# Gates and branch outputs of a hybrid mixer by rows, 512 weight columns at a time, and a transposed merge

## The chip, the cores and the metric

The kernel runs on one core of one Trainium2 chip. The metric is the device time of one execution in microseconds, median of three runs. Five engines work side by side: TensorE (PE in the rows; its weight loads are PEld), VectorE (DVE), ScalarE (ACT), GpSimd (POOL), and SyncE (SP), which issues the DMA transfers here.

## The reference, cut to what matters

Two layers work on 256 tokens of 1024 channels in fp32. In each, the mixer combines an attention branch and a Hyena branch (long convolutions) by sigmoid gates:

```python
y_att = o_att.astype(u.dtype) @ w_o_attn            # (256, 512) @ (512, 1024)
...
y_hy = z @ w_o_hyena                                # (256, 1024) @ (1024, 1024)
gates = jax.nn.sigmoid((u @ w_gate + b_gate).astype(jnp.float32)).reshape(B, S, N_BRANCH, D_MODEL)
merged = gates[:, :, 0] * y_att.astype(jnp.float32) + gates[:, :, 1] * y_hy.astype(jnp.float32)
return merged.astype(u.dtype) @ w_out               # (256, 1024) @ (1024, 1024)
```

`w_gate` has 2048 columns. A normalisation, a residual, and a SwiGLU block follow.

## The kernel before

**Products.** Every fp32 operand `x` of a large product is split into a rounded part `hi` and a remainder `lo`, and a product is three matmuls that add up in one PSUM bank, hi·hi, hi·lo and lo·hi (`mm3`, L80). The activations are kept transposed, channels on partitions, as pairs such as `UH`, `UL` (normalised input), `ZH`, `ZL` (Hyena), `OTH`, `OTL` (attention) and `MH`, `ML` (merged).

**Weights.** They come in pieces of 128 x 1024 (`raw`, 512 KB, four buffers, `RAW`), issued by SP in the order of use. ScalarE rounds a piece (`whi`, L86), VectorE forms the remainder (`wlo`, L89), and every fifth remainder goes to GpSimd (`POOL_LO`). `piece()` keeps three split pieces ahead of TensorE (`AHEAD`).

**Order.** TensorE's order is the program's. On the other engines a scheduler sets it. The mixer runs, in this order: q, k and v of two head slots; 24 pieces of Hyena projections; 16 pieces of gates; two more head slots; 8 pieces of the Hyena output; 4 pieces of the attention output; 8 pieces of the output projection. After almost every piece `tick()` advances up to two background generators by a step: the attention of a slot (`attend`, L609), the convolutions of a channel block (`conv`, L538), or the filters.

**Gates and outputs by columns.** For each block of 128 output columns (`c`), the weight piece is the stationary operand or the moving one in 128 x 128 blocks, and the result is a bank of 128 channels x 256 tokens. Gates: `UH`/`UL` and `whi`/`wlo` give 24 matmuls of 256 columns, and ScalarE applies the sigmoid with the bias of the channel (`bgt`) from the bank into `GT` (L725). The Hyena output multiplies its half of the gates (L750). The attention output, half a piece for a block, multiplies the other half (L766), GpSimd adds both (L767), ScalarE and VectorE split the sum into `MH` and `ML`, and `row_proj` (L429) uses these as stationary operand, with 512 columns of weights moving. There the first two pieces serve both halves of the tokens, the last six the first half first and the second half later.

Of the kernel before, what the change touches and what calls it, by code (L numbers as in the profile page):

```python
# [20 lines left out]
F32 = mybir.dt.float32  # L21
# [6 lines left out]
P = 128  # L28
D = 1024
L = 256  # L30
# [14 lines left out]
def trunk(tc, nc, a, out):  # L45
# [4 lines left out]
    with es:  # L50
# [11 lines left out]
        def bigt(dt=F32, name="big"):  # L62
            return big.tile([P, 1024], dt, tag="big", bufs=22, name=name)
# [16 lines left out]
        def mm3(o, lh, ll, rh, rl, start, stop):  # L80
            mm(o, lh, rh, start, False)
            mm(o, lh, rl, False, False)
            mm(o, ll, rh, False, stop)
# [111 lines left out]
        rope = cst.tile([P, 2, 2, 48], F32, name="rope")  # L195
        mask = cst.tile([P, 2, 512], BF16, name="mask")
        cw = cst.tile([P, DEPTH, 24, 4], F32, name="cw")
        bgt = cst.tile([P, DEPTH, 16], F32, name="bgt")
        fpar = cst.tile([P, DEPTH, 4], F32, name="fpar")
        fc = bigt(name="fc")  # L200
        zT = fc[0:33, 0:256]
# [7 lines left out]
        def load_filter_consts():  # L209
            nc.sync.dma_start(zT, a["zT"])  # L210
            nc.sync.dma_start(fw1, a["fw1"])
            nc.sync.dma_start(fw2, a["fw2"])
            nc.sync.dma_start(fpar, a["fpar"])
            nc.sync.dma_start(bgt, a["bg"])

        def load_consts():
            nc.sync.dma_start(cw, a["cw"])
# [203 lines left out]

        def rows_of(U, o, i, pc, kk, n):

            for k in range(2):
                kt = 2 * kk + k
                w = slice(k * n, (k + 1) * n)
                mm3(o[:, :n], *u_cols(U, kt, i), pc[0][:, w], pc[1][:, w], kt == 0, kt == KT - 1)

        def row_proj(l, n, left, gn, nxt):  # L429


            banks = [[acc() for h in range(2)] for i in range(2)]
            g = g2 = None

            def part(k, i, pc, lr, hs=(0, 1)):
                for h in hs:
                    mm3(banks[i][h], lr[0][:, i * P:(i + 1) * P], lr[1][:, i * P:(i + 1) * P],
                        pc[0][:, HALF[h]], pc[1][:, HALF[h]], k == 0, k == n - 1)

            held = []  # L440
            tail = TAIL if nxt else LAST
            for k in range(n):
                shared[0] = k < n - tail - 2
                pc, lr = piece(), left(k)
                part(k, 0, pc, lr)
                if k < n - tail:
                    part(k, 1, pc, lr)
                    done(pc)
                    tick()
                else:  # L450
                    held.append((k, pc, lr))
                if k == max(0, n - tail - 3):
                    g, g2 = gain(l, gn), gain(*nxt) if nxt else None
            with ordered():
                ss = new_sums()
                for h in range(2):
                    square_sum(ss, h, banks[0][h])
                r = rstd_of(ss)
                if nxt:
                    split_hi()  # L460
                    for q in range(RAW + 1):
                        load(q >= RAW)
                    split_hi()
                add_to_x(0, [times_gain(banks[0][h], g, h) for h in range(2)], r)
                if nxt:
                    split_lo()
                    r = x_rstd(0)
                    split_lo()
                    u0 = pre_b(0, r, g2)
                else:  # L470
                    nc.sync.dma_start(out[0:P, :], X[0])
                ss, t, U = new_sums(), [], None
                for h in range(2):
                    for k, pc, lr in held:
                        if nxt and h and k == n - 2:
                            U = new_U()
                            to_cols(0, u0, U)
                        part(k, 1, pc, lr, (h,))
                    square_sum(ss, h, banks[1][h])
                    t.append(times_gain(banks[1][h], g, h))  # L480
                for _, pc, _ in held:
                    done(pc)
                r = rstd_of(ss)
                if not nxt:
                    add_to_x(1, t, r)
                    for s in HALF:
                        nc.sync.dma_start(out[P:2 * P, s], X[1][:, s])
                    return None, None

                def second():  # L490
                    split_hi()
                    add_to_x(1, t, r)
                    split_lo()
                    ss2 = new_sums()
                    for h in range(2):
                        square_sum(ss2, h, X[1][:, HALF[h]])
                    split_hi()
                    r2 = rstd_of(ss2)
                    split_lo()
                    return pre_b(1, r2, g2)  # L500

                S = start(U, second)
                shared[0] = True
                return U, S
# [168 lines left out]
        def mixer(l, U, o, K):  # L673
# [46 lines left out]

                queue.append(both())

            GT = [bigt(name="GT") for h in range(4)]
            for c in range(16):
                nc.scalar.activation(ct(GT, c), col_proj(U), AF.Sigmoid, bias=bgt[:, l, c:c + 1])  # L725
                tick()
            ZH, ZL = [], []

            def z_split():
# [9 lines left out]
                att = slot(s, [bigt(name="qk") for i in range(2)], z_split if s == 3 else None)  # L739
                queue.append(att)  # L740

            for c in range(8):
                pc = piece()
                wh, wl = pc[:2]
                o = acc()
                for k in range(KT):
                    s = slice(k * P, (k + 1) * P)
                    mm3(o[:, :L], wh[:, s], wl[:, s], ct(ZH, k), ct(ZL, k), k == 0, k == KT - 1)
                done(pc)
                vtt(ct(GT, 8 + c), ct(GT, 8 + c), o[:, :L], op=OP.mult)  # L750
                tick()
            drain()
            MH = [bigt(F32R, name="MH") for h in range(2)]
            ML = [bigt(F32R, name="ML") for h in range(2)]
            for c in range(8):
                if c % 2 == 0:
                    pc = piece()
                    wh, wl = pc[:2]
                o = acc()
                for k in range(4):  # L760
                    s = slice((c % 2) * 512 + k * P, (c % 2) * 512 + (k + 1) * P)
                    mm3(o[:, :L], wh[:, s], wl[:, s], ct([OT[0]], k), ct([OT[1]], k), k == 0, k == 3)
                if c % 2:
                    done(pc)
                g0 = ct(GT, c)
                vtt(g0, g0, o[:, :L], op=OP.mult)  # L766
                ptt(g0, g0, ct(GT, 8 + c), op=OP.add)  # L767
                hi_of(ct(MH, c), g0)
                lo_of(ct(ML, c), g0, ct(MH, c))
            return row_proj(l, KT, lambda k: (ct(MH, k), ct(ML, k)), 1, (l, 2))  # L770


        def ffn(l, U, o):
# [28 lines left out]
            def left(f):  # L802
                hs = r512("hs") if f % 2 else sm.tile([P, 512], F32R, tag="hs", bufs=5, name="hs")
                hi_of(hs[:, :L], ct(HF, f))
                lo_of(hs[:, L:], ct(HF, f), hs[:, :L])
                return hs[:, :L], hs[:, L:]

            return row_proj(l, NF, left, 3, (l + 1, 0) if l + 1 < DEPTH else None)

# [84 lines left out]
    return w.reshape(k // P, P, n // P, P).transpose(2, 1, 0, 3).reshape(n // P, P, k)  # L894


def _pack(i):
    d = _tables()
    d["x"] = np.ascontiguousarray(i["x"][0][PERM])
# [4 lines left out]
    for l in range(DEPTH):  # L904
        win = i["w_in"][l]
        hv, x1, x2 = (_col_pieces(win[:, 4608 + q * D:4608 + (q + 1) * D]) for q in range(3))
        for cc in range(4):
            c = slice(2 * cc, 2 * cc + 2)
            wa[l, PC_H + 6 * cc:PC_H + 6 * cc + 6] = np.concatenate([hv[c], x1[c], x2[c]])
        wa[l, PC_G:PC_G + 16] = _col_pieces(i["w_gate"][l])  # L910
        wa[l, PC_OH:PC_OH + 8] = _col_pieces(i["w_o_hyena"][l])
        wa[l, PC_OA:PC_OA + 4] = _col_pieces(i["w_o_attn"][l]).reshape(4, 2, P, 512).transpose(0, 2, 1, 3).reshape(
            4, P, 1024)
        wa[l, PC_OUT:PC_OUT + 8] = i["w_out"][l].reshape(8, P, D)
        gu = i["w_gate_up"][l].reshape(D, 2, D_FF)
        wg[l] = gu[:, :, :384].reshape(4, 2, P, 2, 384).transpose(3, 0, 2, 1, 4).reshape(8, P, 768)
        for q in range(2):
            wa[l, PC_GU + q:PC_DN:2] = _col_pieces(gu[:, q, 384:])
        wa[l, PC_DN:PC_DN + NF] = i["w_down"][l].reshape(NF, P, D)
        q = win[:, :4608].reshape(4, 2, P, 3, 3, 4, P)  # L920
        wq[l] = q.transpose(5, 3, 0, 2, 1, 4, 6).reshape(48, P, 768)
    d["wa"], d["wq"], d["wg"] = wa, wq, wg
    cwb = np.concatenate([i["conv_w"], i["conv_b"][:, None, :]], 1)
    d["cw"] = np.ascontiguousarray(cwb.reshape(DEPTH, 4, 24, P).transpose(3, 0, 2, 1))
    d["bg"] = np.ascontiguousarray(i["b_gate"].reshape(DEPTH, 16, P).transpose(2, 0, 1))
    fp = np.stack([i["filt_b1"], i["filt_freq1"], i["filt_b2"], i["filt_freq2"]], -1)
    d["fpar"] = np.ascontiguousarray(np.concatenate([fp, fp], 1).transpose(1, 0, 2))
    d["fw1"] = np.ascontiguousarray(i["filt_w1"].transpose(1, 0, 2))
# [31 lines left out]
```

## Time and profile before

| | us |
|---|---|
| median of three runs | 1107.41 (1107.06 to 1108.79) |
| the profiled execution | 1109.53 |
| its span, first to last instruction | 1107.6 |
| TensorE matmul busy in it | 1083.8 |
| VectorE, ScalarE, GpSimd busy | 709.9, 557.1, 396.9 |

Busy time of matmuls is modelled and overlaps, so what one costs is read from the distance between the starts of neighbours. Of layer 0, the gates (with the convolutions' steps among them) lie at 176 to 240 us, the Hyena output at 308 to 337, the attention output at 337 to 349, the output projection from 349 on.

### The profile page before, as it was taken

What the parts mean: (1) busy time and instruction counts of PE and PEld (TensorE: products, weight loads), DVE (VectorE), ACT (ScalarE), POOL (GpSimd) and SP (SyncE); (2) the same over time, 40 slices, a digit from 0 to 9 for tenths busy, and PEclk for the clock granted to TensorE, in tenths of its full rate; (3) what the DMA queues carried; (4) which work ended last, traced back from release to release, by engine and by line L of the source; (5) the groups of instructions that cost most, each with busy time, mean ns of one, the idle gap of its engine ahead of it and who ended that gap; (6) DMA issues with size and microseconds to landing.
All of it is one profiled execution on the core that took longest, in us unless ns stands there. A gap on an engine that the chain in (4) does not pass through costs nothing.

```text
span 1107.6 us, 19530 instructions
## 1 busy us (share of the span) xinstructions
PE 1083.8 (98%) x7624; PEld 1039.0 (94%) x7624; DVE 709.9 (64%) x1139; ACT 557.1 (50%) x852; POOL 396.9 (36%) x488
## 2 busy tenths in 40 slices
PE   8989999999999999999999999999999999999997
PEld 6989999999899899998879899999999989999986
DVE  5799985556647756665474877865545586554554
ACT  6555564443545645454464564454356455544442
POOL 2643133468614134211115714455645230111110
PEclk9999999999999999999999999999999999999999
DMA  8565544434446555656655454444355475465662
GB/s 295 174 211 193 159 138 134 133 117 128 148 143 201 186 188 185 192 182 223 193 169 165 144 166 134 136 151 131 122 162 196 149 232 190 151 183 182 197 199 79
DMA packets 59878, 187.21 MB, mean 169 GB/s; under 512 B 6919, under 2 KB 9353, under 8 KB 59786
## 3 DMA queue, kind: packets, MB, share of 16 engines
q1 hardware_dynamic: 59786, 185.96, 52.6%
q8 instruction: 60, 0.98, 0.4%
q14 instruction: 32, 0.26, 0.1%
HBM read 184.89 MB, written 1.05 MB: 168 GB/s over the span
## 4 chain that ended last, share of the span: by engine, by line
PE 87%; DVE 6%; DMA 3%; ACT 2%; issue 1%; POOL 1%; SPq 0%; DVEq 0%; POOLq 0%; ACTq 0%
PE acc L78 84%; DVE wlo L89 2%; PE acc L617 1%; DVE dl L89 1%; ACT whi L86 1%; DVE dd L315 1%; DMA mask<-in_mask_dram 1%; DMA raw<-in_wq_dram 1%; ACT jk L352 1%; DMA raw<-in_wa_dram 1%; PE acc L647 1%; PE acc L548 1%; PE acc L397 1%; DVE arg L241 0%; DMA w<-in_w_dram 0%
## 5 line engine op out<-in xcount | busy, mean ns | idle before, releaser
L86 ACT ACTIVATE whi<-raw 128x1024 fp32r<-128x1024 f32 (+1 forms) x352 | 345.4, 989 | 384.5 <-PE acc L78 292.6
L89 DVE TENSOR_TENSOR wlo<-raw,whi 128x1024 fp32r<-128x1024 f32 (+1 forms) x294 | 346.4, 1186 | 231.7 <-ACT whi L86 229.2
L78 PE MATMUL acc<-UH,whi 128*128 128x256 f32 x1248 | 356.0, 285 | 0.0
L78 PE MATMUL acc<-UH,wlo 128*128 128x256 f32 x1248 | 353.1, 283 | 0.0
L78 PE MATMUL acc<-UL,whi 128*128 128x256 f32 x1248 | 353.0, 283 | 0.0
L89 POOL TENSOR_TENSOR wlo<-raw,whi 128x1024 fp32r<-128x1024 f32 (+1 forms) x58 | 133.3, 2298 | 412.1 <-ACT whi L86 412.0
L78 PEld LDWEIGHTS acc<-UL,whi 128*128 128x128 f32 x1248 | 239.3, 192 | 0.4
L78 PEld LDWEIGHTS acc<-UH,whi 128*128 128x128 f32 x1248 | 239.2, 192 | 0.4
L78 PEld LDWEIGHTS acc<-UH,wlo 128*128 128x128 f32 x1248 | 239.2, 192 | 0.0
L78 PE MATMUL acc<-wlo,UH 128*128 128x384 f32 x448 | 152.4, 340 | 2.4 <-DVE wlo L89 1.3
L78 PE MATMUL acc<-whi,UH 128*128 128x384 f32 x448 | 153.8, 343 | 0.0
L78 PE MATMUL acc<-whi,UL 128*128 128x384 f32 x448 | 151.1, 337 | 0.0
L78 PE MATMUL acc<-whi,hs 128*128 128x512 f32 x352 | 108.9, 389 | 0.0
L78 PEld LDWEIGHTS acc<-wlo,UH 128*128 128x128 f32 x448 | 85.3, 190 | 5.7 <-DVE wlo L89 4.1
L78 PEld LDWEIGHTS acc<-whi,UH 128*128 128x128 f32 x448 | 85.5, 191 | 1.3 <-ACT whi L86 0.4
L78 PEld LDWEIGHTS acc<-whi,UL 128*128 128x128 f32 x448 | 85.1, 190 | 0.2 <-DVE UL L89 0.2
L78 PEld LDWEIGHTS acc<-whi,hs 128*128 128x128 f32 x352 | 66.1, 188 | 13.6
L78 PE MATMUL acc<-wlo,hs 128*128 128x512 f32 x176 | 68.6, 390 | 0.5 <-DVE wlo L89 0.5
L799 DVE TENSOR_TENSOR HF<-acc,silu 128x256 f32<-128x256 f32 x38 | 16.1, 424 | 49.1 <-PE acc L78 49.1
L359 POOL TENSOR_SCALAR nv<-ss 128x1 f32<-128x1 f32 x16 | 7.0, 440 | 103.7 <-ACT jk L352 103.7
L78 PEld LDWEIGHTS acc<-wlo,hs 128*128 128x128 f32 x176 | 33.0, 188 | 7.7 <-DVE wlo L89 0.9
L89 DVE TENSOR_TENSOR hs<-HF,hs 128x256 fp32r<-128x256 f32 x44 | 31.1, 724 | 10.3 <-ACT hs L86 10.3
(165 smaller groups left out, 1678.9 us busy)
## 6 DMA issues: line engine op xcount, KB each, us to landing
raw<-in_wa_dram SPq DMA_DIRECT2D x240, 512.0 KB, 3.6
raw<-in_wq_dram SPq DMA_DIRECT2D x96, 384.0 KB, 3.2
raw<-in_wg_dram SPq DMA_DIRECT2D x16, 384.0 KB, 3.8
w<-in_w_dram SPq DMA_DIRECT2D x16, 256.0 KB, 4.3
gain<-in_gains_dram SPq DMA_DIRECT2D x7, 512.0 KB, 6.2
dec<-in_dec_dram SPq DMA_DIRECT2D x8, 256.0 KB, 3.8
bb<-in_hyb_dram SPq DMA_DIRECT2D x16, 128.0 KB, 4.0
dftraw<-in_dft_dram SPq DMA_DIRECT2D x3, 256.0 KB, 4.4
```

What stands on the lines that cost most here:

```text
L78: nc.tensor.matmul(o, lT, r, start=start, stop=stop)
L86: return nc.scalar.activation(o, i, AF.Copy)
L89: (eng or nc.vector).tensor_tensor(o, i, h, op=OP.subtract)
L315: vtt(d[:, q * 256:(q + 1) * 256], h[:, q * 256:(q + 1) * 256], dec[:, e, :], op=OP.mult)
L352: nc.scalar.activation(jk, half, AF.Square, scale=D ** -0.5, accum_out=ss[:, h:h + 1])
L359: nc.gpsimd.tensor_scalar(v, ss[:, 0:1], ss[:, 1:2], EPS, op0=OP.add, op1=OP.add)
L397: nc.tensor.transpose(t[:, q * P:(q + 1) * P], u[:, h * 512 + q * P: h * 512 + (q + 1) * P], ident)
L548: nc.tensor.transpose(t[:, q * P:(q + 1) * P], eo[:, q // 2, q % 2, :], ident)
L617: nc.tensor.transpose(t[:, q * P:(q + 1) * P], qk[i][:, j * 384 + g * P: j * 384 + (g + 1) * P], ident)
L647: nc.tensor.transpose(t[:, q * P:(q + 1) * P], S[:, i * 512 + q * P:i * 512 + (q + 1) * P], ident)
L799: vtt(ct(HF, f), ob, sl, op=OP.mult)
```

## The change

The gates, the Hyena output and the attention output are computed by rows. Two banks hold 128 tokens x 512 columns each, one for each half `i` of the tokens; 128 x 128 blocks of the activations are the stationary operand and 512 columns of weights move. A piece of weights covers 256 input channels x 512 columns, so four pieces make a chunk of gates or of the Hyena output and two a chunk of the attention output. The bias is now a row, loaded with the same value for all partitions (`gb`, 256 KB, two buffers shared with the filters' decay windows `dec`), which VectorE adds from the bank into `GT`; ScalarE applies the sigmoid there. The merged sum lies with tokens on partitions and is turned by TensorE (`turn`), 8 transposes for each half of the columns; ScalarE and VectorE split the transposed bank into `MH` and `ML`. The first half is turned inside the last attention piece, the second before the third piece of the output projection. The bytes of weights and the number of ticks stay.

```diff
-            GT = [bigt(name="GT") for h in range(4)]
-            for c in range(16):
-                nc.scalar.activation(ct(GT, c), col_proj(U), AF.Sigmoid, bias=bgt[:, l, c:c + 1])
-                tick()
+            GT = [[bigt(name="GT") for i in range(2)] for b in range(2)]
+            for c in range(4):
+                gb = sm.tile([P, 512], F32, tag="dec", bufs=2, name="gb")
+                nc.sync.dma_start(gb, a["bg"][l, c * 512:(c + 1) * 512].partition_broadcast(P))
+                o = [acc() for i in range(2)]
+                for kk in range(4):
+                    pc = piece()
+                    for i in range(2):
+                        rows_of(U, o[i], i, pc, kk, 512)
+                    done(pc)
+                    tick()
+                for i in range(2):
+                    gt = GT[c // 2][i][:, HALF[c % 2]]
+                    vtt(gt, o[i], gb, op=OP.add)
+                    nc.scalar.activation(gt, gt, AF.Sigmoid)
...
-            for c in range(8):
-                pc = piece()
-                wh, wl = pc[:2]
-                o = acc()
-                for k in range(KT):
-                    s = slice(k * P, (k + 1) * P)
-                    mm3(o[:, :L], wh[:, s], wl[:, s], ct(ZH, k), ct(ZL, k), k == 0, k == KT - 1)
-                done(pc)
-                vtt(ct(GT, 8 + c), ct(GT, 8 + c), o[:, :L], op=OP.mult)
-                tick()
+            for c in range(2):
+                o = [acc() for i in range(2)]
+                for kk in range(4):
+                    pc = piece()
+                    for i in range(2):
+                        rows(lambda k: [ct(T, k)[:, i * P:(i + 1) * P] for T in (ZH, ZL)], o[i], pc, kk, 512, KT)
+                    done(pc)
+                    tick()
+                for i in range(2):
+                    g1 = GT[1][i][:, HALF[c]]
+                    vtt(g1, g1, o[i], op=OP.mult)
             drain()
...
+            def turn(c):
+
+                M[c] = bigt(F32R, name="MH"), bigt(F32R, name="ML")
+                for i in range(2):
+                    t = acc()
+                    for q in range(4):
+                        nc.tensor.transpose(t[:, q * P:(q + 1) * P],
+                                            GT[0][i][:, c * 512 + q * P:c * 512 + (q + 1) * P], ident)
+                    h, lo = (x[:, HALF[i]] for x in M[c])
+                    hi_of(h, t)
+                    lo_of(lo, t, h)
+
+            for c in range(2):
+                o = [acc() for i in range(2)]
+                for kk in range(2):
                     pc = piece()
...
+                    for i in range(2):
+                        if c and kk and i:
+                            turn(0)
+                        rows(lambda k: [T[:, k * L + i * P:k * L + (i + 1) * P] for T in OT], o[i], pc, kk, 512, 4)
                     done(pc)
...
+                for i in range(2):
+                    g0 = GT[0][i][:, HALF[c]]
+                    vtt(g0, g0, o[i], op=OP.mult)
+                    ptt(g0, g0, GT[1][i][:, HALF[c]], op=OP.add)
+
+            def merged(k):
+                if k == 2:
+                    turn(1)
+                return [x[:, :].rearrange("p (i q n) -> p i q n", i=2, q=4)[:, :, k % 4, :] for x in M[k // 4]]
+
+            return row_proj(l, KT, merged, 1, (l, 2))
```

What this does to the order of the instructions is seen at three places of layer 0. TensorE before, at the end of the attention output and the start of the output projection:

```order
L78 MATMUL acc<-OTH,whi 128x256
L78 MATMUL acc<-OTL,whi 128x256
L78 MATMUL acc<-OTH,wlo 128x256
L78 MATMUL acc<-whi,MH 128x512
L78 MATMUL acc<-wlo,MH 128x512
```

And in the changed kernel, where `ident` is the identity matrix of a transpose:

```order
L78 MATMUL acc<-whi,OTL 128x512
L774 MATMUL acc<-ident,GT 128x128 x8
L78 MATMUL acc<-whi,OTH 128x512
L78 MATMUL acc<-wlo,OTH 128x512
L78 MATMUL acc<-whi,OTL 128x512
L78 MATMUL acc<-whi,OTH 128x512
L78 MATMUL acc<-wlo,OTH 128x512
L78 MATMUL acc<-whi,OTL 128x512
L78 MATMUL acc<-whi,MH 128x512
L78 MATMUL acc<-wlo,MH 128x512
```

Six matmuls of the attention output stand between the first eight transposes and the output projection that needs their result. VectorE before, from the last Hyena product (L750) through the attention output:

```order
L750 TENSOR_TENSOR GT<-GT,acc 128x256
L766 TENSOR_TENSOR GT<-GT,acc 128x256 x2
L89 TENSOR_TENSOR wlo<-raw,whi 128x1024
L766 TENSOR_TENSOR GT<-GT,acc 128x256
L89 TENSOR_TENSOR ML<-GT,MH 128x256
L766 TENSOR_TENSOR GT<-GT,acc 128x256
```

The same place in the changed kernel, from the last Hyena products (L764) to the second half of the merge:

```order
L764 TENSOR_TENSOR GT<-GT,acc 128x512 x2
L89 TENSOR_TENSOR wlo<-raw,whi 128x1024
L791 TENSOR_TENSOR GT<-GT,acc 128x512 x2
L89 TENSOR_TENSOR wlo<-raw,whi 128x1024 x2
L791 TENSOR_TENSOR GT<-GT,acc 128x512
L89 TENSOR_TENSOR ML<-acc,MH 128x512 x2
L791 TENSOR_TENSOR GT<-GT,acc 128x512
L89 TENSOR_TENSOR wlo<-raw,whi 128x1024 x3
L89 TENSOR_TENSOR ML<-acc,MH 128x512 x2
```

The remainder of the first half (`ML`) stands behind two weight splits and behind the multiply (L791) of the second chunk's first half of tokens. On SP's queue the bias rows stand among the weights (`raw`), the filters' windows (`dec`) and biases (`bb`); before:

```order
L284 DMA w_1521<-in_w_dram 128x512
L287 DMA dec<-in_dec_dram 128x512
L291 DMA bb<-in_hyb_dram 128x256
L140 DMA raw<-in_wa_dram 128x1024
L291 DMA bb<-in_hyb_dram 128x256
L140 DMA raw<-in_wa_dram 128x1024 x4
L287 DMA dec<-in_dec_dram 128x512
```

And in the changed kernel:

```order
L282 DMA w_1519<-in_w_dram 128x512
L727 DMA gb<-in_bg_dram 128x512
L289 DMA bb<-in_hyb_dram 128x256
L140 DMA raw<-in_wa_dram 128x1024
L289 DMA bb<-in_hyb_dram 128x256
L140 DMA raw<-in_wa_dram 128x1024 x4
L727 DMA gb<-in_bg_dram 128x512
```

The two loads of layer 1's windows moved behind the gates' weights, and two bias rows stand in their place.

## Rows read from the trace of the kernel before

**Rows 1.** The page: busy us (share of the span) x instructions.

```profile
PE 1083.8 (98%) x7624; PEld 1039.0 (94%) x7624; DVE 709.9 (64%) x1139; ACT 557.1 (50%) x852; POOL 396.9 (36%) x488
```

**Rows 2.** Windows of layer 0: busy us by engine, granted clock, DMA share, GB/s.

```profile
176.00:240.00 64.00, 64.00 (x526) 63.97 (x525) 33.04 (x52) 28.27 (x44) 34.03 (x36) 1.00 0.42 130
...
300.00:320.00 20.00, 17.62 (x131) 17.31 (x130) 10.38 (x14) 8.49 (x13) 2.69 (x2) 0.91 0.45 147
320.00:338.00 18.00, 18.00 (x154) 18.00 (x154) 9.68 (x19) 7.35 (x11) 2.54 (x3) 1.00 0.49 157
338.00:349.00 11.00, 11.00 (x93) 11.00 (x92) 8.21 (x13) 5.50 (x9) 8.28 (x7) 1.00 0.43 144
349.00:369.00 20.00, 20.00 (x89) 16.54 (x89) 16.25 (x21) 12.61 (x22) 5.83 (x7) 1.00 0.80 259
```

**Rows 3.** The chain that ended last, layer 1: start us, us, what.

```profile
852.46 0.87 PE acc L617 x8
853.33 2.87 PE acc L78 x24
```

**Rows 4.** Timeline of TensorE, layer 0: start us, us, instruction.

```profile
337.31 0.28 PE L78 MATMUL acc<-OTH,whi 128*128 128x256 f32 x1
...
348.71 0.28 PE L78 MATMUL acc<-OTH,wlo 128*128 128x256 f32 x1
348.83 0.40 PE L78 MATMUL acc<-whi,MH 128*128 128x512 f32 x1
...
369.26 1.31 PE L397 MATMUL acc<-ident,u 128*128 128x128 f32 x8
```

**Rows 5.** Groups by shape: xcount | busy us, mean ns | idle before, releasers.

```profile
L86 ACT ACTIVATE whi<-raw 128x1024 fp32r<-128x1024 f32 x240 | 252.7, 1059 | 301.9 <-PE acc L78 226.9 <-issue 63.0 <-DMA raw<-in_wa_dram 4.2
L89 DVE TENSOR_TENSOR wlo<-raw,whi 128x1024 fp32r<-128x1024 f32 x197 | 247.9, 1264 | 154.5 <-ACT whi L86 152.1 <-issue 2.0
...
L367 DVE TENSOR_TENSOR pn<-acc,gain 128x512 f32<-128x512 f32 x16 | 11.0, 691 | 9.0 <-ACT jk L352 9.0
...
L89 DVE TENSOR_TENSOR UL<-acc,UH 128x512 fp32r<-128x512 f32 x16 | 10.6, 688 | 1.2 <-ACT UH L86 0.7 <-PE acc L397 0.2
...
L86 ACT ACTIVATE UH<-acc 128x512 fp32r<-128x512 f32 x16 | 9.1, 596 | 10.0 <-PE acc L397 9.4 <-PE acc L78 0.5
```

**Rows 6.** Instructions on GT: xcount, ns min/median/max, first and last start.

```profile
L725 ACT ACTIVATE GT<-acc,bgt x32: 453/457/475, 178.1 to 790.9; 128x256 f32<-128x256 f32 x32
...
L767 POOL TENSOR_TENSOR GT<-GT x16: 737/924/1732, 340.9 to 892.0; 128x256 f32<-128x256 f32 x16
L86 ACT ACTIVATE MH<-GT x16: 400/417/419, 341.7 to 893.7; 128x256 fp32r<-128x256 f32 x16
L89 DVE TENSOR_TENSOR ML<-GT,MH x16: 411/633/960, 343.0 to 894.2; 128x256 fp32r<-128x256 f32 x16
```

**Rows 7.** Timelines of VectorE, GpSimd and TensorE around 300 us.

```profile
298.59 0.48 DVE L639 TENSOR_SCALAR S<-S,rd 128x512 f32<-128x512 f32 x1
...
300.72 1.99 DVE L639 TENSOR_SCALAR S<-S,rd 128x512 f32<-128x512 f32 x1
...
299.87 2.55 POOL L89 TENSOR_TENSOR wlo<-raw,whi 128x1024 fp32r<-128x1024 f32 x1 [0.73 <-ACT whi L86]
...
299.52 0.33 PE L78 MATMUL acc<-wlo,UH 128*128 128x384 f32 x1
299.70 0.34 PE L78 MATMUL acc<-whi,UL 128*128 128x384 f32 x1
...
302.85 1.09 PE L647 MATMUL acc<-ident,S 128*128 128x128 f32 x4 [2.38 <-DVE S L639]
303.59 0.67 PE L78 MATMUL acc<-whi,UH 128*128 128x384 f32 x1
304.06 0.52 PE L78 MATMUL acc<-wlo,UH 128*128 128x384 f32 x1
...
305.66 0.43 PE L78 MATMUL acc<-whi,UH 128*128 128x384 f32 x1
```

More of the change, by code (lines that the diff above doesn't have):

```diff
@@ L197, in trunk @@
         cw = cst.tile([P, DEPTH, 24, 4], F32, name="cw")
-        bgt = cst.tile([P, DEPTH, 16], F32, name="bgt")
         fpar = cst.tile([P, DEPTH, 4], F32, name="fpar")
@@ L213, in load_filter_consts @@
             nc.sync.dma_start(fpar, a["fpar"])
-            nc.sync.dma_start(bgt, a["bg"])
         def load_consts():
@@ L422, in rows_of, with rows @@
         def rows_of(U, o, i, pc, kk, n):
+            rows(lambda k: u_cols(U, k, i), o, pc, kk, n, KT)
+        def rows(left, o, pc, kk, n, kts):
             for k in range(2):
@@ L426, in rows_of @@
                 w = slice(k * n, (k + 1) * n)
-                mm3(o[:, :n], *u_cols(U, kt, i), pc[0][:, w], pc[1][:, w], kt == 0, kt == KT - 1)
+                mm3(o[:, :n], *left(kt), pc[0][:, w], pc[1][:, w], kt == 0, kt == kts - 1)
         def row_proj(l, n, left, gn, nxt):
@@ L436, in part @@
                 for h in hs:
-                    mm3(banks[i][h], lr[0][:, i * P:(i + 1) * P], lr[1][:, i * P:(i + 1) * P],
+                    mm3(banks[i][h], lr[0][:, i, :], lr[1][:, i, :],
                         pc[0][:, HALF[h]], pc[1][:, HALF[h]], k == 0, k == n - 1)
@@ L740, in mixer @@
                 queue.append(att)
-            for c in range(8):
-                pc = piece()
-                wh, wl = pc[:2]
-                o = acc()
-                for k in range(KT):
-                    s = slice(k * P, (k + 1) * P)
-                    mm3(o[:, :L], wh[:, s], wl[:, s], ct(ZH, k), ct(ZL, k), k == 0, k == KT - 1)
-                done(pc)
-                vtt(ct(GT, 8 + c), ct(GT, 8 + c), o[:, :L], op=OP.mult)
-                tick()
-            drain()
-            MH = [bigt(F32R, name="MH") for h in range(2)]
@@ L754, in mixer @@
-            ML = [bigt(F32R, name="ML") for h in range(2)]
-            for c in range(8):
-                if c % 2 == 0:
-                    pc = piece()
[L758 to L763, printed above, removed]
-                    done(pc)
[L765 to L769, printed above, removed]
@@ L770, in mixer @@
-            return row_proj(l, KT, lambda k: (ct(MH, k), ct(ML, k)), 1, (l, 2))
+            for c in range(2):
[9 more added lines that the diff above has]
+                    vtt(g1, g1, o[i], op=OP.mult)
@@ new lines, in mixer @@
+            drain()
+            M = [None, None]
+            def turn(c):
[8 more added lines that the diff above has]
+                    lo_of(lo, t, h)
@@ L805, in left @@
                 lo_of(hs[:, L:], ct(HF, f), hs[:, :L])
-                return hs[:, :L], hs[:, L:]
+                return [x.rearrange("p (i n) -> p i n", i=2) for x in (hs[:, :L], hs[:, L:])]
             return row_proj(l, NF, left, 3, (l + 1, 0) if l + 1 < DEPTH else None)
@@ L894, in _col_pieces, with _row_pieces @@
     return w.reshape(k // P, P, n // P, P).transpose(2, 1, 0, 3).reshape(n // P, P, k)
+def _row_pieces(w):
+    k, n = w.shape
+    return w.reshape(k // 256, 2, P, n // 512, 512).transpose(3, 0, 2, 1, 4).reshape(k * n // (P * 1024), P, 1024)
 def _pack(i):
@@ L909, in _pack @@
             wa[l, PC_H + 6 * cc:PC_H + 6 * cc + 6] = np.concatenate([hv[c], x1[c], x2[c]])
[L910 to L913, printed above, removed]
+        wa[l, PC_G:PC_G + 16] = _row_pieces(i["w_gate"][l])
+        wa[l, PC_OH:PC_OH + 8] = _row_pieces(i["w_o_hyena"][l])
+        wa[l, PC_OA:PC_OA + 4] = _row_pieces(i["w_o_attn"][l])
         wa[l, PC_OUT:PC_OUT + 8] = i["w_out"][l].reshape(8, P, D)
@@ L924, in _pack @@
     d["cw"] = np.ascontiguousarray(cwb.reshape(DEPTH, 4, 24, P).transpose(3, 0, 2, 1))
-    d["bg"] = np.ascontiguousarray(i["b_gate"].reshape(DEPTH, 16, P).transpose(2, 0, 1))
+    d["bg"] = np.ascontiguousarray(i["b_gate"])
     fp = np.stack([i["filt_b1"], i["filt_freq1"], i["filt_b2"], i["filt_freq2"]], -1)
```

## The prediction

> **What bounds the kernel now.** The busy line comes first: TensorE is busy for 98% of the span, VectorE 64%, ScalarE 50%, GpSimd 36% [rows 1]. A busy matmul line alone proves little, so the windows of layer 0 come next, cut at the stages that the diff touches. From 176 to 240 us (the gates, with convolutions between them) TensorE has not one idle moment, and the other three are busy for about half; it is as full in the Hyena output (320 to 338), the attention output (338 to 349) and the output projection (349 to 369). Only 300 to 320 shows a hole, and there the granted clock falls to 0.91 [rows 2]. The chain of work that ended last in layer 1 says the same: matmul after matmul, no other engine among them [rows 3]. So in these stages the time is the sum of what TensorE needs per instruction, and whatever the others do is free while it is ready in time.
>
> What an instruction costs is read from start to start, not from the durations, which overlap. In the attention output the first 256-column matmul starts at 337.31 and the first 512-column matmul behind that stage at 348.83: 96 matmuls in 11.52 us, 120.0 ns each. From 348.83 to the transposes at 369.26 stand 90 matmuls of 512 columns: 20.43 us, 227.0 ns each [rows 4]. Twice the columns cost 1.89 times as much. The chain agrees: 24 matmuls in 2.87 us [rows 3].
>
> **The change, part by part.** *Fewer, wider matmuls.* A layer has 16 gate pieces and 8 Hyena pieces of 24 matmuls, and 4 attention pieces of 24: 28 x 24 = 672 of 256 columns. They become 28 x 12 = 336 of 512. Per layer 672 x 0.1200 = 80.64 us against 336 x 0.2270 = 76.27 us: 4.37 us saved, 8.74 us in both layers.
>
> The Trainium skill, page "TensorE: Matmul & The Clock Gate", section "Back-to-back issue gap", gives a gap of N/2.4 + 2.5 ns at the full clock: it leaves only 2.5 ns of fixed cost, where the rows leave 2 x 120.0 - 227.0 = 13 ns. By the page the wider matmuls would return 672 x 2.5 ns = 1.7 us, an estimate, and the change would lose. [...] I go by the rows.
>
> *Transposes.* Each layer gains 4 groups of 4 transposes, in two runs of eight. Eight transposes took 0.87 us on the path [rows 3]. Two runs, two layers: 3.48 us added. Their evacuations replace others: ScalarE rounds 512 columns from a bank in 0.60 us and VectorE takes the remainder in 0.69 [rows 5], 4 of each where there were 8 of 0.42 and 0.63 us [rows 6]. VectorE and ScalarE have room, so this is zero unless it is late (below).
>
> *Gates.* ScalarE loses 16 sigmoids of 0.457 us a layer [rows 6] and gets 8 of some 0.6 us (as its 512-column copy [rows 5]); VectorE gets 8 bias additions from a bank of about 0.69 us [rows 5], 5.5 us in a stage of 64 us in which it was busy for 33 [rows 2]. A sigmoid now waits for VectorE, which waits for the end of a chunk of four pieces; behind it on ScalarE stand the next weights' roundings. Three pieces are split ahead, 3 x 2.72 = 8.2 us of TensorE work, against a delay of some 1.3 us: hidden. The convolutions between the pieces have 2 x 0.156 = 0.3 us less cover per two pieces; none of their waits was on the path from 176 to 240 [rows 2]. Zero, with 1 us as the far end.
>
> *Bias rows.* Eight loads of 256 KB stand in SP's queue among the weights. In layer 0 the first two stand where layer 1's decay windows did; the others wait for a multiply two chunks back and can hold the weights behind them for about one piece, 2.7 us, with seven pieces in flight. The queues moved 130 to 157 GB/s in these stages and 259 behind them [rows 2], so there is room: zero. The load of bias columns that goes away at the start counts nothing either: no matmul of the first 170 us needs it.
>
> *The merge* is the only place with a thin margin. Count from the first attention matmul. TensorE reaches the first run of transposes after 42 matmuls, at 42 x 0.227 = 9.53 us, its second half at 9.97. The operands are the first 512 columns: VectorE's two multiplies (0.69 each) follow the matmuls at 4.09 and 5.45 us, then GpSimd adds. A 256-column addition there took 0.737 to 1.732 us, median 0.924 [rows 6]; the trace has none of this kind with 512 columns, so I bound one by twice those: 1.47 to 3.46, and take the median, 1.85, since a weight split runs beside them now as before. In front of the multiplies VectorE has a weight split, whose buffer comes back after 12 matmuls: 2.72 + 1.06 + 1.26 [rows 5] = 5.0, the first multiply ends at 5.7, and the two additions at 8.7 to 12.7 us, by the median 9.4: 0.6 us early, at worst 2.7 us late. Next, the output projection's third matmul, at 9.53 + 0.87 + 1.36 + 0.45 = 12.2 us, needs the remainder ML. VectorE's row, in the order shown above, has a weight split and a multiply in front of it. That split cannot start before its rounding, which waits for a buffer that TensorE returns after 36 matmuls (8.17): 8.17 + 1.06 + 1.26 = 10.5 [rows 5]; multiply 11.2; ML 11.9. It is 0.3 us early. The second run of transposes comes 24 matmuls (5.4 us) after its operands' matmuls, against 0.69 + 2 x 1.85: early by about 1 us. With margins this thin I charge 0.4 us a layer: 0.8 us.
>
> Sum: -8.74 + 3.48 + 0.8 = **-4.5 us**. The profiled execution took 1109.53 us (span 1107.6 and 1.9 around it), 2.1 us above the median; what is saved is matmul pacing, which the span shows at full clock almost throughout, so the difference is taken from the median 1107.41: **1102.9 us**.
>
> **Rivals.** *The merge waits (same).* GpSimd's additions at their slowest leave TensorE idle for 2.7 us a layer at the second half of the first transposes. The trace shows what comes with that: at 302.85 TensorE had waited 2.38 us for VectorE, whose scaling took 1.99 us instead of 0.48 while GpSimd split a weight in 2.55; behind it 384-column matmuls take five steps from 304.06 to 305.66, 0.32 us each, where they had taken 0.18 [rows 7]. That is the granted clock at its lower level, 1.2 GHz, and over seven such steps and the transposes (0.74 us for four, where eight take 0.87) it lost about 1.4 us. The matmuls and transposes sum to -5.3; half of the worst case, 1.35 us a layer, leaves -2.6, 1104.8 us, and all of it without the clock +0.1, 1107.5. For it speaks that the longest addition did take 1.73 us, against it the median of 0.92 [rows 6].
>
> *Slower.* The same place, but with the clock's fall: 2.7 + 1.4 us a layer, 8.2 us, gives +2.9 us, 1110.3. It decides only when the second addition ends 2.3 us after TensorE arrives, in both layers; each addition would then take 3.3 us, nearly twice the longest seen.
>
> *The hole at 300 closes too (faster).* That wait of 2.38 us hung on one GpSimd split meeting one VectorE scaling; the stages ahead of it now end earlier and their splits stand differently. Without it and its clock: 3.8 us more, -8.3, 1099.1 us. Against it: the number of pieces, the split's turn and the order from the second gate chunk on are unchanged, so the two should meet again.
>
> *The width returns nothing (slower).* If a 512-column matmul of these stages took twice the 120 ns of a 256-column one, 240 ns, nothing would be saved, and the transposes alone would count: +3.5 us, 1110.9. The rows speak against it: in the output projection strips of the same shape move, at 227 ns. The skill's formula above would end between, at -1.7 + 3.5 = +1.8 us, 1109.2, an estimate.
>
> That nothing changes because TensorE is not what bounds these stages is excluded by [rows 2]; that the matmuls really halve stands in the order.
>
> **Chances.** My forecast 0.55, the merge waits 0.20, the merge with the clock's fall 0.05, the hole closes 0.15, no return of the width 0.05. A run of this kernel is told from no change beyond about 0.2%, 2.2 us: below 1105.2 is faster. The forecast and the closed hole lie there, and about a quarter of the waiting case (up to 1.2 us a layer): 0.75. The rest of that case is the same, 0.15. The two slower cases hold 0.10. The range reaches from the closed hole to near the end of the waiting case: 1099.0 to 1107.0; the forecast alone holds 1101.2 to 1104.5 (1 us of shorter waits elsewhere beside -5.3, to 2.4 us of new ones).
>
> **What would show it.** Right: 512-column matmuls of gates, Hyena and attention 227 ns apart; runs of eight transposes in 0.87 us; TensorE without idle time in the gates; additions of 1.5 to 2.3 us that end before the transposes. Wrong: a gap of TensorE at the transposes with GpSimd as releaser, or at the output projection's third matmul with VectorE; a granted clock below 1.00 behind it; a spacing above 235 ns; a convolution's transposes or inverse waiting for GpSimd in the gate stage; weights late behind a bias load.

## The result, and the profile after

The changed kernel took 1101.53 us (median of 5 runs, 1101.19 to 1103.01) beside 1107.41 for the kernel before (5 runs, 1106.99 to 1108.79): a ratio of 0.9945, 95% interval 0.9931 to 0.9960, 5.9 us faster. The forecast was 1102.9 us. A second comparison, below, gave 0.9930 (0.9913 to 0.9947), 7.7 us. The two agree within their intervals, and both lie beyond what the changed instructions themselves explain: 4.0 us, as shown below.

The page of the changed kernel, its profiled execution 1101.53 us long with a span of 1099.8:

```profile
PE 1077.7 (98%) x6984; PEld 1005.5 (91%) x6984; DVE 712.9 (65%) x1131; ACT 554.0 (50%) x828; POOL 394.1 (36%) x480
```

TensorE has 640 matmuls fewer than in [rows 1] (672 of 256 columns fewer per layer, 336 of 512 and 16 transposes more) and is as full as it was. The windows of layer 0, columns as in [rows 2]:

```profile
176.00:238.00 62.00, 62.00 (x346) 54.46 (x346) 39.08 (x61) 26.99 (x35) 33.92 (x36) 1.00 0.48 150
297.00:317.00 20.00, 17.61 (x105) 15.60 (x104) 10.60 (x13) 9.62 (x14) 3.57 (x3) 1.00 0.50 158
317.00:333.00 16.00, 16.00 (x85) 13.57 (x83) 9.53 (x15) 6.65 (x10) 2.15 (x3) 1.00 0.45 145
333.00:345.00 12.00, 12.00 (x59) 10.03 (x57) 7.22 (x9) 5.35 (x6) 6.58 (x4) 1.00 0.56 175
345.00:367.00 22.00, 22.00 (x105) 18.04 (x104) 16.22 (x20) 12.69 (x22) 5.49 (x6) 1.00 0.75 242
```

TensorE is without a gap in the gates, both branch outputs and the output projection. The hole is still there (297 to 317 has 17.61 us of work in 20), but the granted clock behind it is 1.00 where [rows 2] had 0.91. The merge, the place with the thin margin, from the timelines of TensorE, GpSimd and VectorE:

```profile
333.00 0.39 PE L78 MATMUL acc<-whi,OTH 128*128 128x512 f32 x1
...
342.52 1.03 PE L774 MATMUL acc<-ident,GT 128*128 128x128 f32 x8
343.31 0.48 PE L78 MATMUL acc<-whi,OTH 128*128 128x512 f32 x1
343.63 0.40 PE L78 MATMUL acc<-wlo,OTH 128*128 128x512 f32 x1
343.86 0.39 PE L78 MATMUL acc<-whi,OTL 128*128 128x512 f32 x1
...
345.22 0.39 PE L78 MATMUL acc<-whi,ML 128*128 128x512 f32 x1
...
338.92 3.53 POOL L792 TENSOR_TENSOR GT<-GT 128x512 f32<-128x512 f32 x2 [2.17 <-DVE GT L791]
344.36 1.30 POOL L792 TENSOR_TENSOR GT<-GT 128x512 f32<-128x512 f32 x1 [1.91 <-DVE GT L791]
346.15 2.35 POOL L792 TENSOR_TENSOR GT<-GT 128x512 f32<-128x512 f32 x1 [0.49 <-DVE GT L791]
...
344.19 1.28 DVE L89 TENSOR_TENSOR ML<-acc,MH 128x512 fp32r<-128x512 f32 x2
```

From the first attention matmul at 333.00 the first two additions begin at 5.92 us and end at 9.45; TensorE arrives at 9.52, and at the second half of the run, which needs the second addition, four transposes later, at 9.96. The prediction had 5.7, 9.4, 9.53 and 9.97. The two ML of the first run take 1.28 us from 344.19, so the first is done near 344.8, and TensorE uses it at 345.22. TensorE waits at neither place. The list of TensorE's waits names neither GpSimd's addition nor ML (releaser: us in total, times, longest):

```profile
PE acc L78 <- DVE dl L89: 6.9, 6, 2.3
PE acc L78 <- DMA grow<-in_gains_dram: 2.4, 1, 2.4
PE acc L648 <- DVE S L640: 2.4, 1, 2.4
```

The first two are filter work and the start of the program, the third is the hole; the kernel before had them too, 7.4, 2.3 and 2.4 us.

**Where the time went.** TensorE's transposes of attention, convolutions and `to_cols` are the same in both kernels and run in the same order, so their starts are marks to compare traces by. The pieces of layer 1's chain between the first and the last transposes of a convolution in the gates, kernel before:

```profile
726.61 0.44 PE acc L548 x4
...
760.28 5.76 PE acc L78 x48
766.03 0.44 PE acc L548 x4
766.47 23.71 PE acc L78 x200
790.19 0.44 PE acc L548 x4
```

The changed kernel:

```profile
720.87 0.44 PE acc L549 x4
...
753.42 5.46 PE acc L78 x24
758.88 0.44 PE acc L549 x4
759.32 22.84 PE acc L78 x128
782.16 0.44 PE acc L549 x4
```

63.58 us have become 61.29, 2.29 less, and in the middle 48 matmuls in 5.76 us have become 24 in 5.46. The same marks over the whole program give this table; each entry is how much longer a stretch took than in the first trace of the changed kernel (stretches by its times; what the rows leave out differs by at most 0.2 us each), for four profiles of the kernel before and a second one of the changed kernel:

| stretch, us | before | again | third | fourth | changed, again |
|---|---|---|---|---|---|
| 7 to 165, start and filters | -0.42 | -3.22 | 1.90 | 0.06 | -0.87 |
| 165 to 238, gates 0 | 2.17 | 2.18 | 2.17 | 2.18 | 0.00 |
| 301 to 308, hole | 1.50 | 0.10 | 1.67 | 1.52 | 1.59 |
| 308 to 366, outputs 0 | -0.29 | -0.28 | -0.29 | -0.28 | 0.03 |
| 366 to 575, FFN 0 | 0.86 | 0.62 | 0.75 | 0.90 | 0.66 |
| 575 to 630, head of mixer 1 | 1.75 | 0.75 | 3.18 | 0.95 | 2.03 |
| 721 to 782, gates 1 | 2.29 | 2.28 | 2.28 | 2.29 | 0.01 |
| 782 to 902, outputs 1 | -0.33 | -0.29 | -0.30 | -0.32 | -0.02 |

What the change touches repeats to 0.05 us: gates -2.2 and -2.3, the outputs with their transposes +0.3 and +0.3, 0.1 at the start of the Hyena output (inside the hole's row); 4.0 us together. The other rows hold the same TensorE instructions in both kernels and vary from one execution to the next by more than that. On SP's queue they are not quite the same: the load of the bias columns is gone from the start, and two loads of layer 1's windows moved.

### The profile page after: what moved, and what is told of

Same layout as the page of the kernel before. It is cut to its first block, busy times and chain, and to the rows that moved or that the text cites. A ratio compares the mean times of both kernels' runs of the same rounds, so it can differ in the third digit from the quotient of the medians.

```text
span 1099.8 us, 18234 instructions
## 1 busy us (share of the span) xinstructions
PE 1077.7 (98%) x6984; PEld 1005.5 (91%) x6984; DVE 712.9 (65%) x1131; ACT 554.0 (50%) x828; POOL 394.1 (36%) x480
## 4 chain that ended last, share of the span: by engine, by line
PE 88%; DVE 6%; DMA 2%; ACT 2%; issue 1%; POOL 1%; SPq 0%; DVEq 0%; POOLq 0%; ACTq 0%
PE acc L78 84%; DVE wlo L89 2%; PE acc L618 1%; DVE dl L89 1%; DMA mask<-in_mask_dram 1%; DVE dd L313 1%; ACT jk L350 1%; DMA raw<-in_wq_dram 1%; ACT whi L86 1%; PE acc L549 1%; PE acc L395 1%; PE acc L648 1%; DVE arg L239 1%; DMA w<-in_w_dram 0%; DVE X L371 0%
## 5 line engine op out<-in xcount | busy, mean ns | idle before, releaser
L78 PE MATMUL acc<-UH,whi 128*128 128x256 f32 x992 | 282.4, 285 | 0.0
L78 PE MATMUL acc<-UH,wlo 128*128 128x256 f32 x992 | 280.6, 283 | 0.0
L78 PE MATMUL acc<-UL,whi 128*128 128x256 f32 x992 | 280.6, 283 | 0.0
L78 PE MATMUL acc<-whi,UH 128*128 128x384 f32 (+1 forms) x576 | 204.6, 355 | 0.0
L78 PE MATMUL acc<-wlo,UH 128*128 128x384 f32 (+1 forms) x576 | 202.0, 351 | 2.2 <-DVE wlo L89 1.4
L78 PE MATMUL acc<-whi,UL 128*128 128x384 f32 (+1 forms) x576 | 200.6, 348 | 0.0
L78 PEld LDWEIGHTS acc<-UL,whi 128*128 128x128 f32 x992 | 190.2, 192 | 0.4
L78 PEld LDWEIGHTS acc<-UH,whi 128*128 128x128 f32 x992 | 190.1, 192 | 0.4
L78 PEld LDWEIGHTS acc<-UH,wlo 128*128 128x128 f32 x992 | 190.1, 192 | 0.0
L567 POOL TENSOR_TENSOR t<-t 128x256 f32<-128x256 f32 x32 | 36.5, 1142 | 4.3 <-DVE t L565 2.3
```

Of the source, the lines that this page charges most:

```text
L78: nc.tensor.matmul(o, lT, r, start=start, stop=stop)
L567: ptt(t1[:, 256:512], t2[:, 0:256], t2[:, 256:512], op=OP.add)
```

## The experiments

Ratios are to the kernel before, run beside them; a difference to a changed kernel that was not run beside them is taken from its second ratio, 0.9930 (by the first, 0.9945, it comes out 1.7 us lower). "Lag" is a difference in the table's sense.

**The kernel before again, three times** (no edit).

> The kernel before, unchanged, for a second profile of it. The profiles show 7.8 us between the two spans, the times 5.9 us. My theory: the matmul widths and the transposes give 4.3 us, and the fall of the granted clock behind the hole at 300 us (1.4 us) and the late weights of layer 0's FFN belong to the one profiled run, not to the kernel; then the new profile has a span of about 1105.5 us, and the clock behind the hole stays at 1.00 or falls as chance has it. Rival: both belong to the kernel before, whose stages stand differently against the weights; then they are there again, and about 1.5 us of the 5.9 us were gained at them.

> The kernel before once more, for the profile. The changed kernel's times are 5.9 to 7.7 us below the kernel before, the stretches that differ by the change 4.0 us in the traces. My theory: the rest is what the kernel before loses, in most of its runs, to falls of the granted clock behind the hole at 300 us and at the head of layer 1's mixer around 610 us (1.4 and 1.7 us each), and to late weights; a span near 1108 us with at least one of these falls. Rival: no fall and a span near 1108 us, with the loss spread over the 256-column stages, or a span near 1104 us.

> As the run before this one, for a fourth profile of the kernel before: the same expectations.

The first repeat was timed at 0.9997 (0.9981 to 1.0012). The spans of the three profiles were 1102.0, 1111.3 and 1107.2 us; over 12 runs the same kernel took 1103.95 to 1112.42. Windows of the third profile of the kernel before (granted clock is the third number from the end):

```profile
305.00:310.00 5.00, 4.95 (x24) 4.98 (x25) 1.64 (x2) 1.72 (x4) 0.00 (x0) 0.66 0.71 221
...
615.00:620.00 5.00, 4.58 (x20) 4.58 (x21) 3.18 (x10) 1.36 (x3) 5.00 (x6) 0.66 0.55 184
```

And of the second, the same kernel:

```profile
305.00:310.00 5.00, 5.00 (x45) 5.00 (x44) 2.31 (x4) 2.03 (x3) 0.00 (x0) 1.00 0.39 113
...
615.00:620.00 5.00, 5.00 (x27) 4.65 (x27) 3.29 (x8) 2.97 (x4) 2.68 (x8) 1.00 0.84 250
```

Behind the hole the clock fell in three of four profiles of the kernel before; the 2.4 us wait itself was in all four. So the fall of [rows 7] belongs to the execution, not to the kernel. The changed kernel shows it in its second profile too (0.66 from 300 to 305). The third profile lies above the span I expected, the second below and the fourth near it.

**The changed kernel again** (no edit).

> The changed kernel, unchanged, beside the kernel before on this chip. The second profile of the kernel before had a span of 1102.0 us, 5.6 us less than the first, so stages that the change does not touch make up several us from run to run. My theory, from the stretches that are at the full clock in the traces compared so far: the change gives 2.0 us a layer, 4.0 us; a ratio of 0.9964. Rival: 5.9 us as first measured, a ratio of 0.9945 or less, with something beside the matmuls and transposes that recurs.

0.9930 (0.9913 to 0.9947): the rival's side. The traces keep to 4.0 us for the touched stretches; the timed runs differ by 2 to 3.7 us more.

**Halves.** Width alone taken back.

```diff
-                mm3(o[:, :n], *left(kt), pc[0][:, w], pc[1][:, w], kt == 0, kt == kts - 1)
...
+                lh, ll = left(kt)
+                for q, (a_, b_) in enumerate(((lh, pc[0]), (lh, pc[1]), (ll, pc[0]))):
+                    if kt == 0 and q == 0:
+                        mm(o, a_, b_[:, w], True, False)
+                        continue
+                    for h in range(2):
+                        m = slice(h * 256, (h + 1) * 256)
+                        mm(o[:, m], a_, b_[:, k * n + h * 256:k * n + (h + 1) * 256], False,
+                           kt == kts - 1 and q == 2 and h == 1)
```

> The changed kernel, but each 512-column matmul of gates, Hyena output and attention output issued as two of 256 columns into the two halves of the same bank, except the first of each bank. 320 matmuls more per layer at the same columns; nothing else moves. My theory (2 x 120.0 - 227.0 = 13 ns per matmul saved): +8.3 us, 1109.8 us. Rival, width returns little (2.5 ns each): +1.6 us, 1103.1 us, and the gain came from the other parts of the change.

1.0012 (0.9999 to 1.0024), 1112.1 us beside 1110.4: the whole gain is gone, and the 1.3 us more are not clear of noise. That is 9.1 us above the changed kernel. The chain of this kernel in layer 1's gates:

```profile
729.24 0.44 PE acc L560 x4
...
762.82 5.73 PE acc L78 x46
...
792.67 0.44 PE acc L560 x4
```

63.43 us where the full width took 61.29. Over both layers it lags by 3.56 and 3.62 us, 7.2 for 640 matmuls: 11.2 ns each, not 13; the other 1.9 us lie in stretches that vary from one execution to the next. Either figure is far from the 1.6 us of the rival. The rival took its 2.5 ns from a formula of the Trainium skill, page "TensorE: Matmul & The Clock Gate", section "Back-to-back issue gap", which the section gives for a single matmul by itself and not for a stream of loads and matmuls; in this stream each matmul more costs over four times that.

**Gates alone.** The kernel before with the new gates loop, the bias rows and row-wise pieces, outputs as they were; gates and outputs then stand in different layouts, so the gating multiplies other pairs of values, as many of them.

```diff
-for c in range(16):
-    nc.scalar.activation(ct(GT, c), col_proj(U), AF.Sigmoid, bias=bgt[:, l, c:c + 1])
+for c in range(4):
...
+                    for i in range(2):
+                        rows_of(U, o[i], i, pc, kk, 512)
...
+                    gt = GT[2 * (c // 2) + i][:, HALF[c % 2]]
+                    vtt(gt, o[i], gb, op=OP.add)
+                    nc.scalar.activation(gt, gt, AF.Sigmoid)
```

> The kernel before with the gates alone computed by rows, 512 columns at a time, with bias rows; the two outputs stay by columns and are multiplied with gates in the other layout. My theory: 192 pairs of matmuls per layer, 384 x 13 ns = 5.0 us (the layer 1 trace of the changed kernel shows 2.3 us a layer, 4.6 us): 1102.4 to 1102.8 us. Rival, width returns little: 384 x 2.5 ns = 1 us, 1106.4 us. If the clock behind the hole at 300 us comes back with this part too, 1.4 us less, 1101.2 us.

0.9950 (0.9931 to 0.9968), 1105.1 us beside 1110.4. The chain in layer 1's gates:

```profile
725.89 0.44 PE acc L546 x4
...
787.18 0.44 PE acc L546 x4
```

61.29 us, the changed kernel's length to the hundredth. So the gates bring all of the 4.0 us and half a microsecond more (2.17 and 2.29 us), and what the outputs save by rows is less than their transposes take.

**No transposes.** The merged rows go straight into the rounding; the output projection multiplies by an operand that is not transposed.

```diff
-t = acc()
-for q in range(4):
-    nc.tensor.transpose(t[:, q * P:(q + 1) * P],
-                        GT[0][i][:, c * 512 + q * P:c * 512 + (q + 1) * P], ident)
+t = GT[0][i][:, HALF[c]]
```

> The changed kernel without its 64 transposes: the merged rows are split as they stand, so the output projection multiplies by an operand that is not transposed. My theory: four runs of 0.87 us lie on TensorE's path and go, -3.5 us, 1098.0 us. Rival, they stand in time that TensorE would have waited for the merge: less than half of that, 1100 us or more, with a wait for GpSimd or VectorE at the output projection's first matmuls.

(The transposes are 32, not 64, here and in the next expectation: four runs of eight, as the sum has them.)

0.9912 (0.9896 to 0.9927), 1100.6 us, about 2 us below the changed kernel. The trace gains 1.87 us in layer 1 and only 1.24 in layer 0, where the chain now leaves TensorE:

```profile
324.56 12.71 PE acc L78 x64
337.29 1.07 ACT whi L86
...
339.86 1.78 DVE ML L89
...
346.25 5.20 DMA raw<-in_wa_dram
...
351.50 1.23 DVE wlo L89
352.77 10.95 PE acc L78 x47
```

A weight's transfer and its split end last there, and TensorE waits 0.33 us for the split at 352.77. So without the transposes some half a microsecond of layer 0 goes to a late weight. The remainders ML also take longer here (two in 1.78 us at 339.86, where the changed kernel took 1.28), so how much of that wait comes from this edit's own work on VectorE is not shown.

**Transposes twice.**

```diff
-for q in range(4):
+for q in (0, 1, 2, 3) * 2:
```

> The changed kernel with each of its 64 transposes issued twice into the same place. My theory: 0.87 us a run, four runs, +3.5 us against the changed kernel. Rival, from the kernel without them, where layer 0 gave back only 1.2 us because weights were late behind VectorE: more time at the transposes lets the splits catch up, and it costs less, +2.5 us.

0.9952 (0.9936 to 0.9969), 2.4 us above the changed kernel run beside the same kernel before, with overlapping intervals. The trace lags by 1.77 and 1.74 us in the two layers, 3.5; each run reads like this in the chain:

```profile
879.01 1.75 PE acc L774 x16
```

Sixteen in 1.75 us, eight in 0.87: the term of the sum.

**A second addition at the merge.**

```diff
+spare = t512("spare")
+ptt(spare, GT[1][i][:, HALF[c]], GT[1][i][:, HALF[c]], op=OP.add)
 ptt(g0, g0, GT[1][i][:, HALF[c]], op=OP.add)
```

> The changed kernel with a second GpSimd addition of the same size, into a spare tile, ahead of each of the four additions of the merge. In the trace of the changed kernel the two additions end 9.45 us after the first attention matmul, and TensorE arrives at 9.52 us and at the second half at about 9.96. My theory, the margin is as thin as that and the additions take 1.77 us here: the first ends 1.8 us late and the second 3.0 us, about 3 us of waiting in each layer, +6 us (up to +9 if the granted clock falls behind it), with GpSimd named as the releaser at the transposes. Rival, there is slack that the sum does not see: +2 us or less.

0.9925 (0.9907 to 0.9943): nothing lost. GpSimd's timeline shows that it was no test:

```profile
331.85 1.04 POOL L793 TENSOR_TENSOR spare<-GT 128x512 f32<-128x512 f32 x1 [10.83 <-DVE GT L764]
...
338.36 3.54 POOL L794 TENSOR_TENSOR GT<-GT 128x512 f32<-128x512 f32 x2 [1.76 <-DVE GT L791]
```

The extra additions read only the gated Hyena output, so they ran 6.5 us ahead of the others, in GpSimd's idle time. In the next experiment they read the product as well:

```diff
+ptt(spare, g0, GT[1][i][:, HALF[c]], op=OP.add)
```

> The test of the merge again. In the run with a second GpSimd addition the scheduler put the extra ones ahead, into idle time of GpSimd, so they delayed nothing. Here the extra addition reads the product of the gate, so that it can't start before it, and GpSimd does two extra and then the two additions of the first run of transposes. My theory, the additions take 1.77 us there and the margin at TensorE is 0.1 to 0.5 us: the first addition ends 11.2 us after the first attention matmul, 1.7 us late, and the second at 13.0, 3.0 us late; TensorE waits about 3 us in each layer, +6 us against the changed kernel, more if the granted clock falls behind the wait. Rival, slack that the sum does not see: +2 us or less.

0.9994 (0.9976 to 1.0013): the whole gain is gone, about 7 us above the changed kernel, as expected. GpSimd's timeline in layer 0:

```profile
339.72 3.53 POOL L793 TENSOR_TENSOR spare<-GT 128x512 f32<-128x512 f32 x2 [2.18 <-DVE GT L791]
343.21 3.46 POOL L794 TENSOR_TENSOR GT<-GT 128x512 f32<-128x512 f32 x2
```

and TensorE's waits name it, four times, which the changed kernel's list does not:

```profile
PE acc L774 <- POOL GT L794: 5.2, 4, 1.6
```

The lag is 3.1 us in layer 0 and 4.7 in layer 1; there the granted clock fell behind the wait:

```profile
885.00:890.00 5.00, 3.44 (x14) 2.73 (x12) 2.62 (x4) 1.19 (x2) 4.35 (x3) 0.71 0.64 184
```

The margin is as thin as worked out, and the rival's mechanism, wait and clock, is real; in the changed kernel it does not happen, by the 0.5 us between 9.45 and 9.96.

**The hole.** The softmax scaling on ScalarE.

```diff
-nc.vector.tensor_scalar(Si, Si, rd, None, op0=OP.mult)
+nc.scalar.activation(Si, Si, AF.Copy, scale=rd)
```

> The changed kernel with the scaling of the softmax rows done by ScalarE and not by VectorE, which needed 1.98 us for it in the hole at 298 us while GpSimd split a weight. My theory: the wait of TensorE there falls from 2.4 to about 0.9 us, and with it the chance of the clock's fall: -1.5 to -2.5 us against the changed kernel. Rival: the sixteen scalings push ScalarE's roundings back, new waits eat it, 0 to +1 us.

0.9923 (0.9907 to 0.9939), 0.8 us below the changed kernel, not to be told from nothing. A smaller wait was left than was there, but not the 0.9 us that I had expected:

```profile
PE acc L648 <- ACT S L640: 1.6, 1, 1.6
```

**The FFN by rows too.** 2048 of the gate and up columns as in the change.

```diff
-for f in range(3, NF):
-    oa, ob = col_proj(U), col_proj(U)
+for c in range(4):
+    for q in range(2):
+        o = [acc() for i in range(2)]
+        for kk in range(4):
+            pc = piece()
+            for i in range(2):
+                rows_of(U, o[i], i, pc, kk, 512)
...
+    turned(c, hn)
```

> The changed kernel with the same turn of the matmuls in the FFN: 2048 of the gate and of the up columns by rows, 512 at a time, the products transposed for the down projection; the last 384 stay by columns. Per layer 32 pieces x 12 x 11.7 ns = 4.5 us less (the saving that the gate stage of layer 1 shows per pair of matmuls), 32 transposes at 109 ns = 3.5 us more: -1.0 us a layer, -2 us against the changed kernel. Rival: the transposes wait for VectorE's products or the copies are late at the down projection, 0 to +3 us.

0.9907 (0.9882 to 0.9932), 1099.2 us beside 1109.4, about 2.5 us below the changed kernel, with overlapping intervals. From the end of mixer 0 to the end of FFN 0 its trace takes 198.4 us against 199.1, and from the end of mixer 1 to the end of the span 195.8 against 197.3: 2.2 us, close to the 2 expected. The 0.7 us of layer 0 is no more than the scatter of FFN 0 in the table; the 1.5 us of layer 1 is clear of it. In this kernel a name used twice makes the first three tiles' transposes read a later chunk's tile: the same instructions on other data. It shows the price of the turn and is no version to use; none with that put right was run.

## Why the prediction was right, step by step

**Bound.** "The time is the sum of what TensorE needs per instruction": held. Gates and outputs changed by their matmuls and transposes alone, the same to 0.05 us in every pair of traces.

**Fewer, wider matmuls, -8.74 us.** Right mechanism, a sixth too large. With the transposes at 3.5 us, the 4.0 us of the touched stretches leave 7.5 us for 672 pairs of matmuls, 11.2 ns a pair, as in the halves; the gates of layer 1 give 2.29 us for 192 pairs, 11.9 ns. The sum had 13 ns, from the spacings in the attention output and the output projection. In the gates, 24 matmuls take 5.46 us where 48 took 5.76, 12.5 ns a pair; in the stretch behind, which the convolutions' own matmuls interrupt, 22.84 us where it was 23.71, 12.1 ns for each of 72 pairs.

**Transposes, +3.48 us.** Right; the doubled ones cost 3.5 us. The first step behind a run is long (343.31 to 343.63, 0.32 us for a step of 0.23), but the run's last step is short: from the start of the run to that second matmul (342.52 to 343.63) 1.11 us pass, 0.88 us more than the one step.

**The merge, +0.8 us charged.** The times of its steps up to the first ML were right within about 0.2 us, and the wait is zero. The two additions together took 3.53 us where the sum had 3.70; a single one took 1.29 to 2.35 us, 1.78 in the median:

```profile
L792 POOL TENSOR_TENSOR GT<-GT x8: 1293/1777/2352, 338.9 to 882.4; 128x512 f32<-128x512 f32 x8
```

The charge stood for a wait that did not come and happened to cover most of what the matmuls saved less: -5.3 + 0.8 = -4.5 was forecast, -4.0 is what the touched stretches show. That the two are so close is luck.

**Gates' other engines, bias rows: zero.** Held; no wait in the gates, and no weight late behind a bias row.

**From 4.0 to 5.9 and 7.7 us.** Not predicted, and not explained; that the first measured time is only 1.4 us from the forecast is in part luck too. Averaged over four profiles of the kernel before and six of the changed kernel and its variants at the merge, start, hole, FFN 0 and head of mixer 1 take 2.3 us longer in the kernel before: 1.0 at the start, 0.1 in the hole, 0.5 in FFN 0, 0.8 at the head. By the scatter of the ten that has a standard error of 2.0 us. One part recurs: at the head of mixer 1 TensorE waits for a split by GpSimd (`sl`) 0.7 to 0.9 us in all four, and 0 to 0.7 us in the six. The kernel before and the changed kernel's second profile:

```profile
PE acc L78 <- POOL sl L89: 0.8, 1, 0.8
...
PE acc L78 <- POOL sl L89: 0.4, 1, 0.4
```

The clock gives a second, different hint. Its granted mean was 0.9948 over the 51 runs of the kernel before that stood beside other kernels (0.9949 with its own repeats) and 0.9965 over the 11 of the changed one, each uncertain by 0.0003; 0.0016 of 1108 us is 1.8 us. But in the ten profiles it was 0.9955 in both groups, so there the 2.3 us are not clock. Whether the moved loads, the clock or chance makes the rest stays open; no run here separates them.

**Rivals.** The merge's wait is one addition away, and would have taken all of the gain. The hole did not close: 2.4 us in every profile of either kernel; only the clock behind it varied. That the width returns nothing is refuted by the halves.

## What to carry to other kernels

In this kernel a change from 256 to 512 columns per matmul is worth some 11 to 12 ns per matmul removed where TensorE is full; where the result must be turned afterwards the transposes eat it (the outputs lost 0.3 us a layer), where it is used elementwise all of it stays (the gates, 2.2 us). Before a difference of a few microseconds is explained, profile the unchanged kernel again and compare the two traces stretch by stretch at instructions that both have: here what the change touched repeated to 0.05 us, while untouched stretches moved by up to 5 us. An extra instruction that is to delay something must depend on what it is to follow, or the scheduler puts it where it costs nothing.

## What the hardware showed that was not expected

The wait in the hole is one engine shut out by another. Timelines of GpSimd, VectorE and TensorE, changed kernel:

```profile
297.98 2.55 POOL L89 TENSOR_TENSOR wlo<-raw,whi 128x1024 fp32r<-128x1024 f32 x1 [0.72 <-ACT whi L86]
...
298.83 1.98 DVE L640 TENSOR_SCALAR S<-S,rd 128x512 f32<-128x512 f32 x1
...
300.96 0.63 PE L648 MATMUL acc<-ident,S 128*128 128x128 f32 x4 [2.39 <-DVE S L640]
```

The scaling, 0.48 us elsewhere, ends 0.28 us after GpSimd's split does (300.53), and in [rows 7] 0.29 us after it (302.71 and 302.42). In both it ends with the split, as if it had stood still for it. The Trainium skill, page "SBUF — State Buffer", section "Who interferes with whom", says that the port pair that VectorE and GpSimd share is locked for a whole instruction, and that the other engine is fully blocked. Both traces agree with that. On ScalarE, beside a split of GpSimd, the scaling took 0.72 us.

After equal waits of 2.4 us the granted clock fell to its lower level in some executions and not in others, of either kernel.
